# A two-layer hybrid diffusion block: norms as one unbroken VectorE sequence, seams reordered

## The chip, the cores and the metric

The kernel runs on one core of a Trainium2 chip. The metric is device time in microseconds (us) of one execution, as the median of several runs. TensorE multiplies matrices, VectorE and ScalarE work element by element, GpSimd and SyncE issue transfers (GpSimd does a little arithmetic as well). In the profile they are called PE, DVE, ACT, POOL and SP.

## The reference

512 latent tokens and 256 context tokens of width 1024 pass through two layers. In each layer the input is normed and modulated, projected once, and the projection is cut into a bidirectional linear recurrence (A), a spatial gating MLP (B), a windowed attention with a sink (C) and three gates. The last layer updates latent tokens alone.

```python
zx = modulate(rms_norm(x, g_norm1[l]), sh1x, sc1x) @ w_in[l]
ya_x = rglru_bidir(zx[..., OFF_A:OFF_B], ...)
yb_x = spatial_gating(gelu(zx[..., OFF_B:OFF_Q]), ...)
yc_x = windowed_attention(q, k, v, kc, vc, sink[l])
x = x + ga1x * merge_branches(zx[..., OFF_G:], ya_x, yb_x, yc_x, w_branch[l], w_out[l])
x = x + ga2x * sq_relu_mlp(modulate(rms_norm(x, g_norm2[l]), sh2x, sc2x), w_ff1[l], w_ff2[l])
```

`rms_norm` divides by the root of the mean square over the 1024 channels of a token. `modulate` is `h * (1 + scale) + shift`, and scale, shift and the gates `ga1`, `ga2` come from a product of the conditioning vector with `w_mod`. Everything is 32-bit floating point.

## The kernel before

**Products.** Channels lie on the 128 partitions, tokens along the free dimension: `self.x` is 8 tiles of 128 channels by 768 tokens (512 in the last layer). A 32-bit product is made of three passes: both operands are split into a high part (a copy rounded to fp32r) and a low part (the rest), and high by high, high by low and low by high are summed in PSUM. A weight block is 128 x 1024 elements. `parted` (L193 and below in `Net`) loads it on SP (`wr<-w`), copies the high part on ACT (`wh<-wr`) and subtracts on DVE (`wl<-wr,wh`). There are three buffers each for `wr`, `wh` and `wl`. One block against one range of tokens is 24 passes of TensorE. 44 blocks of layer 1 (`EARLY`, the four key/value blocks first) are split ahead of time during the MLP of layer 0, stored by GpSimd as `hd` and `ld`, and later loaded back by SP straight into `wh` and `wl`.

**Order.** Nothing is issued as the code is read. Each call is recorded, and `schedule` then plans all five engines: at each moment an engine takes the recorded operation with the best priority that is ready by the planner's costs, fits the buffers, and lies within `far` (275) operations of the oldest unfinished one. A transfer is taken to land 1900 ns after its bytes have passed at 360 bytes/ns. `emit` issues the planned order, so every instruction of the trace has one source line, L508. Calls within `bundle()` are planned as one piece, with nothing of the same engine between them. In `rsqrt` (nine to twelve tiny DVE operations, Newton's method) only the tags in `CHAINS` are bundled.

**Norms.** `rms` sums squares: ACT squares, DVE adds over the 8 tiles, PE adds over partitions (matmuls of one column). On DVE follow the mean, the root, and for every 128 tokens one diagonal matrix (`s<-ident,t`). PE spreads the diagonals over the partitions with a matmul by ones (`p<-s,ones`). `norm` then multiplies by that and by the gain (DVE, `s<-s,G,p`), and ACT and DVE make the high and low parts that the next product reads. Between the diagonals and the first product of the next stage lies that whole chain.

**Seams.** To give TensorE work in the meantime, the two products next to a norm run on one range of tokens after the other ("streams", `streams(W)`: 512 and 256 tokens in layer 0, 256 and 256 in layer 1). `out_proj` does 2 of its 8 blocks on all tokens at once and 6 per stream, and norms a stream when it is done. `ff` does the first group of four blocks of its first matrix per stream, everything in the middle on all tokens, and in layer 0 the last group `ff2(7)` per stream, each followed by the norm of layer 1; then come the keys and values of layer 1 (`kv_proj`). Between the streams of a seam the same weight block is loaded and split anew.

**Other work in the gaps.** `merge` adds the three gated branch projections. DVE also computes the modulation of later stages as 128 dot products of a row of `w_mod` with the conditioning vector (`junk<-wr,condb`, the row loaded by SP as `wr<-wmod`). `layer_consts` loads and prepares the recurrence's constants of a layer, and `kv_post` calls it at the layer's start.

Of the kernel before, what the change touches and what calls it, by code (L numbers as in the profile page):

```python
# [19 lines left out]
F32R = mybir.dt.float32r  # L20
# [3 lines left out]
OP = mybir.AluOpType  # L24
# [33 lines left out]
LAZY = 200  # L58
DRAINS = 50
FULL, URGENT = 6, 150  # L60
WINDOW = 275
TABLES = {"Sigmoid": (2,), "Sqrt": (3,), "Gelu_apprx_tanh": (11,), "Exp": (0,), "Tanh": (0, 2, 11)}

# [119 lines left out]
class Rec:  # L183
# [153 lines left out]
    def schedule(self):  # L337
# [90 lines left out]
        while events:  # L428
            now = events[0][0]
            while events and events[0][0] <= now + 1e-6:  # L430
                _, _, kind, x = heapq.heappop(events)
                if kind == "rel":
                    used[x.tag] -= 1
                    places[x.tag].append(x)
                    live[x.tag][x.first:x.last + 1] -= 1
                    if x.early:
                        early[x.tag][x.early[0]:x.early[1]] -= 1
            for e in range(5):
                while free[e] <= now + 1e-6:
                    best = pick(e)  # L440
                    if best is None:
                        break
                    _, j, i = best
                    cand[e].pop(j)
                    op = ops[i]
                    for b in op.new:
                        if b.space == "dram":
                            continue
                        used[b.tag] += 1
                        b.early = None  # L450
                        b.prev = places[b.tag].pop(0)
                        if b.prev is None:
                            b.place = fresh[b.tag]
                            fresh[b.tag] += 1
                        else:
                            b.place = b.prev.place
                        if b.first > front:
                            b.early = (front, b.first)
                            early[b.tag][front:b.first] += 1
                    dur = op.dur  # L460
                    if op.both and free[POOL] > now and busy:
                        dur += free[POOL] - now
                    if e == POOL:
                        busy = not op.nbytes
                    if e == ACT and op.table and table not in op.table:
                        dur += 1283
                        table = op.table[0]
                    free[e] = now + dur
                    end = now + dur
                    if op.nbytes:  # L470
                        dma = max(dma, end) + op.nbytes / 360.0
                        end = dma + 1900
                    op.end = end
                    for b in op.psum:
                        b.acc[e] = end
# [46 lines left out]
AHEAD_C = ('', '0', '1', '2', 'k', '')  # L522
AHEAD_X = ('', '0', '1', 'k')
NEAR = 60
JOINT = (2,)
EARLY = [*range(B_K, B_F2), *range(B_G, B_P), *range(B_AX, B_V)]


# [1 line left out]
class Net:  # L530
# [43 lines left out]
    def weights(self, l, blk):  # L574
        rec = self.rec
        rec.boost, was = self.wboost, rec.boost
        if (l, blk) in self.stored:
            hi = self.wtile("wh", [128, 1024], F32R)
            lo = self.wtile("wl", [128, 1024], F32R)
            for t, d in zip((hi, lo), self.stored[l, blk]):  # L580
                rec.sync.dma_start(t.bitcast(F32), d.bitcast(F32))
        else:
            hi, lo = self.parted(l, blk)
        rec.boost = was
        return hi, lo
# [67 lines left out]
    def begin(self, hs):  # L653
# [8 lines left out]
        G = self.hold([128, 2, KT], F32, name="G00", tag="G0")  # L662
        ps = [self.p1() for _ in range(6)]
        self.wboost = 0
        for k in range(KT):
            if k % 2 == 0:
                p = self.mod_rows(k // 2)
                w = self.weights(0, B_K + k // 2)
            nc.vector.tensor_scalar(G[:, :, k], p[:, 2 * (k % 2):2 * (k % 2) + 2], bm[:, k:k + 1],
                                    vec[:, V_G1 + k:V_G1 + k + 1], op0=OP.add, op1=OP.mult)  # L670
# [142 lines left out]

    def rms(self, parts, adder=None):
        nc = self.nc
        sums = []
        for i, (a, b) in enumerate(parts):
            S = self.slot([128, b - a])
# [14 lines left out]
                                     start=True, stop=True)  # L833
                    n += 1
        v = self.tiny(nt, "nv")
        nc.vector.tensor_scalar(v, ps[:, :nt], 1.0 / D, EPS, op0=OP.mult, op1=OP.add)
        rs = self.rsqrt(v, nt, "n")
        out = []
        n = 0
        for a, b in parts:  # L840
            dg = self.slot([128, b - a])
            for i in range((b - a) // 128):
                nc.vector.tensor_scalar(dg[:, i * 128:(i + 1) * 128], self.ident, rs[:, n:n + 1], None, op0=OP.mult)
                n += 1
# [106 lines left out]
    def kv_post(self, l, ps, pairs):  # L951
        nc = self.nc
        if pairs[0] == 0:
            self.layer_consts(l)
            self.kr, self.VS = [], []
        n = 8 * len(pairs)
        ss = self.tiny(n, "kss")
# [443 lines left out]
    def ff(self, l, hs, W):  # L1401
        nc = self.nc

        def ff1(c, parts):
            out = [(self.slot([128, W], F32R), self.slot([128, W], F32R)) for _ in range(4)]
            for z in parts:
                for j in range(4):
                    w = self.weights(l, B_F1 + 4 * c + j)
                    if len(parts) == 1:
                        self.ahead()  # L1410
                    ps = self.fm(w, hs, z)
                    for p, a, b in ps:
                        r = self.slot([128, b - a])
                        nc.scalar.activation(r, p, AF.Relu)
                        nc.vector.tensor_mul(r, r, r)
                        self.split(r, out[j][0][:, a:b], out[j][1][:, a:b])
            return out

        def ff2(c, z, parts):
            for j in range(4):  # L1420
                w = self.weights(l, B_F2 + 4 * c + j)
                if c < 7:
                    self.ahead()
                for i in range(2):
                    ps = self.fm(w, z, parts, kk=4, off=i * 128, stride=256)
                    self.residual(l, 40, ps, 2 * j + i)

        z = ff1(0, [[q] for q in self.streams(W)])
        self.aside = False
        for c in range(7):  # L1430
            for _ in range(3):
                self.bg()
            z2 = ff1(c + 1, [self.parts(W)])
            ff2(c, z, self.parts(W))
            z = z2
        if l == DEPTH - 1:
            ff2(7, z, self.parts(W))
            return
# [7 lines left out]
        for toks in (range(4), range(4, 6)):  # L1446
            self.kv_proj(l + 1, hs, ps, toks)
            self.kv_post(l + 1, ps, (0, 1) if toks[0] == 0 else (2,))
        return hs, ps

    def run(self):
        nc, t = self.nc, self.t
        self.setup()
        hs = self.pairs(TOK)
        ps = self.begin(hs)
        self.consts()
        self.xsrc = t["x"]
        for l in range(DEPTH):
            last = l == DEPTH - 1
# [141 lines left out]
```

## Time and profile before

| | |
|---|---|
| median of 3 runs | 2654.45 us (2653.88 to 2655.54) |
| profiled execution | 2655.47 us, span 2653.7 us |
| TensorE busy | 2604.5 us, 98% of the span |
| VectorE, ScalarE, GpSimd busy | 1840.1, 1200.1, 122.7 us |
| mean granted TensorE clock | 0.995 of full speed |
| 336 loads `wr<-w` of 512 KB | 3.8 us from issue to landing (median) |
| transfers | 403.54 MB, 152 GB/s over the span |

Times are from the start of the span. A row of the timeline gives start, duration, engine, source line, operation, output and inputs, shape and count; in brackets stands how long the engine had been idle before it and what ended that. Buffer numbers are left out there, so that all weight blocks read `wl<-wr,wh`. "Granted clock" is TensorE's clock in parts of full speed; its two levels are 1.2 and 2.4 GHz, that is 0.5 and 1.0. `SPq` is the transfer itself, `SP` its issue.

### The profile page before, as it was taken

What the parts mean: (1) busy time and instruction counts of PE and PEld (TensorE: products, weight loads), DVE (VectorE), ACT (ScalarE), POOL (GpSimd) and SP (SyncE); (2) the same over time, 40 slices, a digit from 0 to 9 for tenths busy, and PEclk for the clock granted to TensorE, in tenths of its full rate; (3) what the DMA queues carried; (4) which work ended last, traced back from release to release, by engine and by line L of the source; (5) the groups of instructions that cost most, each with busy time, mean ns of one, the idle gap of its engine ahead of it and who ended that gap; (6) DMA issues with size and microseconds to landing.
All of it is one profiled execution on the core that took longest, in us unless ns stands there. A gap on an engine that the chain in (4) does not pass through costs nothing.

```text
span 2653.7 us, 38578 instructions
## 1 busy us (share of the span) xinstructions
PE 2604.5 (98%) x14916; PEld 2246.2 (85%) x14916; DVE 1840.1 (69%) x3504; ACT 1200.1 (45%) x1987; POOL 122.7 (5%) x217
## 2 busy tenths in 40 slices
PE   7999999999999999999999989999999999999999
PEld 4989988888898888888888878888887888888887
DVE  8888776997637748465666678886986567844444
ACT  4566557993122225332333334667993233532322
POOL 1000000011000000100111000000011000000000
PEclk9999999999999999999999999999999999999999
DMA  6122213466425424766778634334577565533332
GB/s 248 45 69 74 61 56 104 122 198 226 154 80 165 162 79 134 230 214 199 246 261 263 207 134 169 105 121 154 159 245 248 165 189 178 158 95 96 95 93 83
DMA packets 129528, 403.54 MB, mean 152 GB/s; under 512 B 15232, under 2 KB 25632, under 8 KB 129344
## 3 DMA queue, kind: packets, MB, share of 16 engines
q1 hardware_dynamic: 99360, 302.11, 36.3%
q0 software_dynamic: 23072, 83.24, 9.4%
q10 hardware_dynamic: 6912, 15.73, 1.6%
q8 instruction: 117, 1.92, 0.3%
q14 instruction: 67, 0.55, 0.1%
HBM read 319.23 MB, written 81.79 MB: 151 GB/s over the span
## 4 chain that ended last, share of the span: by engine, by line
PE 69%; DVE 6%; ACT 3%; issue 1%; DMA 1%; ACTq 0%; DVEq 0%; POOLq 0%
PE p L508 69%; DVE s L508 4%; ACT s L508 3%; DVE wl L508 1%; DMA wr<-wmod 1%; DVE t L508 1%; ACT L508 0%; ACT wh L508 0%; DMA ya<-s 0%; DVE junk L508 0%; ACTq L508 0%; DVEq L508 0%; POOLq L508 0%
## 5 line engine op out<-in xcount | busy, mean ns | idle before, releaser
L508 PE MATMUL p<-s,wh 128*128 128x512 f32 (+1 forms) x6816 | 1670.7, 353 | 8.8 <-DVE s L508 6.1
L508 PEld LDWEIGHTS p<-s,wh 128*128 128x128 f32 x6816 | 1192.0, 189 | 239.7 <-DVE s L508 7.8
L508 PE MATMUL p<-s,wl 128*128 128x512 f32 (+1 forms) x3408 | 1028.5, 351 | 8.8 <-DVE wl L508 8.8
L508 ACT ACTIVATE wh<-wr 128x1024 fp32r<-128x1024 f32 x336 | 354.8, 1059 | 871.7 <-PE p L508 475.0
L508 PEld LDWEIGHTS p<-s,wl 128*128 128x128 f32 x3408 | 570.3, 189 | 58.2 <-DVE wl L508 11.1
L508 DVE TENSOR_TENSOR wl<-wr,wh 128x1024 fp32r<-128x1024 f32 x336 | 409.7, 1222 | 291.8 <-ACT wh L508 249.6
L508 ACT ACTIVATE s<-p 128x512 f32<-128x512 f32 (+6 forms) x598 | 282.0, 511 | 271.1 <-PE p L508 255.2
L508 PE MATMUL p<-wh,s 128*128 128x256 f32 (+1 forms) x1472 | 301.9, 298 | 1.7 <-DVE s L508 1.0
L508 DVE TENSOR_TENSOR s<-s,s 128x512 fp32r<-128x512 f32 (+5 forms) x361 | 258.1, 728 | 53.4 <-ACT s L508 49.0
L508 PE MATMUL p<-s,s 128*128 128x256 f32 (+3 forms) x1568 | 279.9, 319 | 5.9 <-ACT s L508 3.9
L508 ACT ACTIVATE s<-s 128x512 fp32r<-128x512 f32 (+6 forms) x301 | 182.5, 633 | 195.7 <-DVE s L508 179.3
L508 PEld LDWEIGHTS p<-s,s 128*128 128x128 f32 (+1 forms) x1568 | 219.5, 183 | 41.0 <-DVE s L508 7.3
L508 PEld LDWEIGHTS p<-wh,s 128*128 128x128 f32 x1472 | 236.3, 188 | 13.7 <-DVE s L508 2.3
L508 DVE SCALAR_TENSOR_TENSOR s<-p,mod,s 128x512 f32<-128x512 f32 (+1 forms) x222 | 138.7, 646 | 156.2 <-PE p L508 155.5
L508 PE MATMUL p<-wl,s 128*128 128x256 f32 (+1 forms) x736 | 217.9, 296 | 1.0 <-DVE wl L508 1.0
L508 DVE SCALAR_TENSOR_TENSOR junk<-wr,condb 128x1024 bf16<-128x1024 f32 x128 | 156.4, 1222 | 86.7 <-DMA wr<-wmod 85.7
L508 DVE TENSOR_TENSOR s<-p,s 128x512 fp32r<-128x512 f32 (+4 forms) x324 | 182.8, 595 | 37.3 <-ACT s L508 31.5
L508 PEld LDWEIGHTS p<-wl,s 128*128 128x128 f32 x736 | 138.5, 188 | 6.6 <-DVE wl L508 1.6
L508 ACT ACTIVATE s<-s,t,t 128x512 f32<-128x512 f32 (+1 forms) x128 | 109.9, 863 | 50.2 <-DVE t L508 49.8
L508 DVE SCALAR_TENSOR_TENSOR s<-s,s 128x768 f32<-128x768 f32 x128 | 116.7, 949 | 16.2 <-ACT s L508 16.2
L508 PE MATMUL p<-ident,s 128*128 128x128 f32 (+1 forms) x776 | 102.9, 274 | 5.2 <-DVE s L508 3.1
L508 PEld LDWEIGHTS p<-ident,s 128*128 128x128 f32 (+1 forms) x776 | 88.4, 142 | 14.1 <-ACT s L508 3.5
(90 smaller groups left out, 1236.2 us busy)
## 6 DMA issues: line engine op xcount, KB each, us to landing
wr<-w SPq DMA_DIRECT2D x336, 512.0 KB, 3.8
wr<-wmod SPq DMA_DIRECT2D x80, 512.0 KB, 4.2
wl<-ld SPq DMA_DIRECT2D x48, 512.0 KB, 4.8
wh<-hd SPq DMA_DIRECT2D x48, 512.0 KB, 3.7
hd<-wh POOLq DMA_DIRECT2D x44, 512.0 KB, 3.7
ld<-wl POOLq DMA_DIRECT2D x44, 512.0 KB, 5.6
gd<-s ACTq DMA_DIRECT2D x24, 384.0 KB, 2.6
s<-gd POOLq DMA_DIRECT2D x24, 384.0 KB, 5.7
```

Source lines behind the costliest of these rows:

```text
L508: ins = getattr(getattr(self.nc, name), method)(*[r(x) for x in a], **{q: r(x) for q, x in k.items()})
```

## The change

1. `rms`: mean, root and all diagonals of a norm are one bundle (`WHOLE`), and the diagonals' buffers are taken first.
2. `schedule`: a transfer is taken to land 2600 ns (SP, ACT) or 4800 ns (POOL) after its bytes, rather than 1900 ns (`LANDS`).
3. `weights`: loads of split key/value blocks are planned only within 160 operations of the oldest unfinished one (`CLOSE`).
4. `ff`: in layer 0 the last seam does blocks 2 and 3 of `ff2(6)` per stream as well (`SPLIT`, `THIRDS`); in layer 1 the first seam also does blocks 0 and 1 of the second column group per stream (`OVER`).
5. `out_proj`: 1 block jointly and 7 per stream, rather than 2 and 6 (`JOINT`).
6. `layer_consts` of layer 1 is called in the middle of layer 0's MLP (`CONSTS`); that of layer 0 and `consts` get a range of 200 rather than 275 (`LATE`).
7. `begin`: the first gain columns are computed ahead of the loop (`LEAD`).

```diff
@@ globals
+LANDS = {SP: 2600, ACT: 2600, POOL: 4800}
-JOINT = (2,)
+CLOSE = 160
+CONSTS = 4
+LEAD = 1
+LATE = 200
+WHOLE = True
+SPLIT = 2
+OVER = (0, 1)
+THIRDS = ((0, 512), (512, 768))
+JOINT = (1,)
@@ schedule
-                        end = dma + 1900
+                        end = dma + LANDS[e]
@@ weights
+            rec.far = CLOSE if B_K <= blk < B_Q else None
             for t, d in zip((hi, lo), self.stored[l, blk]):
                 rec.sync.dma_start(t.bitcast(F32), d.bitcast(F32))
+            rec.far = None
@@ begin
+        for pair in range(LEAD):
+            scales(pair)
         for k in range(KT):
             if k % 2 == 0:
-                p = self.mod_rows(k // 2)
+                if k // 2 >= LEAD:
+                    scales(k // 2)
                 w = self.weights(0, B_K + k // 2)
@@ rms
-        nc.vector.tensor_scalar(v, ps[:, :nt], 1.0 / D, EPS, op0=OP.mult, op1=OP.add)
-        rs = self.rsqrt(v, nt, "n")
+        dgs = [self.slot([128, b - a]) for a, b in parts]
...
+        with self.rec.bundle() if whole else nullcontext():
+            if whole:
+                nc.vector.tensor_scalar(v, ps[:, :nt], 1.0 / D, EPS, op0=OP.mult, op1=OP.add)
+                rs = self.rsqrt(v, nt, "nn")
+            n = 0
+            for dg, (a, b) in zip(dgs, parts):
+                for i in range((b - a) // 128):
+                    nc.vector.tensor_scalar(dg[:, i * 128:(i + 1) * 128], self.ident, rs[:, n:n + 1], None, op0=OP.mult)
+                    n += 1
@@ kv_post
-            self.layer_consts(l)
+            if l == 0:
+                self.rec.far = LATE
+                self.layer_consts(l)
+                self.rec.far = None
@@ ff
-        z = ff1(0, [[q] for q in self.streams(W)])
+        z, z1 = room(), room() if l == DEPTH - 1 else None
+        for q in self.streams(W):
+            ff1(0, [q], z)
+            if z1:
+                ff1(1, [q], z1, OVER)
...
+            if c == CONSTS and l < DEPTH - 1:
+                rec = self.rec
+                rec.boost, was = -LAZY, rec.boost
+                self.layer_consts(l + 1)
+                rec.boost = was
+            if c == 0 and z1:
+                z2 = ff1(1, self.parts(W), z1, [j for j in range(4) if j not in OVER])
+            else:
+                z2 = ff1(c + 1, self.parts(W), room())
+            ff2(c, z, self.parts(W), range(4) if c < 6 or l == DEPTH - 1 else range(SPLIT))
+            z, z6 = z2, z
...
-        for q in self.streams(W):
+        for q in THIRDS:
+            ff2(6, z6, [q], range(SPLIT, 4))
             ff2(7, z, [q])
             self.norm(l + 1, 0, hs, G, *q)
```

What this does to the order of the instructions is seen best at three places. The first is SP's queue at the seam between the layers. `wr` are blocks of the last MLP group, `ld_112`, `hd_112` and the next numbers the parts of the stored key/value blocks. Before:

```order
L508 DMA wr_14727<-w 128x1024
L508 DMA wr_14765<-w 128x1024
L508 DMA wl_14789<-ld_112_10941 128x1024
L508 DMA wh_14793<-hd_112_10919 128x1024
L508 DMA wr_14821<-w 128x1024
L508 DMA wl_14877<-ld_113_11019 128x1024
L508 DMA wr_14949<-w 128x1024
L508 DMA wr_14988<-w 128x1024
L508 DMA wr_15028<-w 128x1024
L508 DMA wr_15068<-w 128x1024
L508 DMA wr_15110<-w 128x1024
L508 DMA wh_15225<-hd_113_11000 128x1024
```

Now:

```order
L509 DMA wr_14919<-w 128x1024
L509 DMA wr_14958<-w 128x1024
L509 DMA wr_14998<-w 128x1024
L509 DMA wr_15040<-w 128x1024
L509 DMA wl_15066<-ld_112_10960 128x1024
L509 DMA wr_15139<-w 128x1024
L509 DMA wl_15166<-ld_113_11038 128x1024
L509 DMA wh_15207<-hd_112_10944 128x1024
L509 DMA wh_15259<-hd_113_11028 128x1024
L509 DMA wh_15381<-hd_114_11110 128x1024
```

The loads of blocks 112 and 113 stood ahead of the last five or six weight loads and now stand among the last two; two more weight blocks are loaded, because two blocks of `ff2(6)` come once per stream.

The second place is DVE at the first norm of layer 1's MLP (the stream of tokens 0 to 255). `t` are mean and root, `s<-ident,t` the diagonals, `wl` splits of weight blocks, `s<-s,G,p` the norm's products. Before, from the root's end on:

```order
L508 SCALAR_TENSOR_TENSOR t_22453<-t_22451,t_22453 128x2
L508 TENSOR_TENSOR wl_22478<-wr_22359,wh_22435 128x1024
L508 TENSOR_SCALAR s_22492<-ident,t_22453 128x128
L508 SCALAR_TENSOR_TENSOR s_21502<-p_22431,mod_10721,s_21502 128x256
L508 TENSOR_SCALAR s_22492<-ident,t_22453 128x128
L508 TENSOR_TENSOR wl_22506<-wr_22394,wh_22487 128x1024
L508 SCALAR_TENSOR_TENSOR s_22516<-s_21496,G_22031,p_22511 128x256
L508 SCALAR_TENSOR_TENSOR s_22523<-s_21498,G_22031,p_22511 128x256
L508 SCALAR_TENSOR_TENSOR s_22530<-s_21500,G_22031,p_22511 128x256
```

Now:

```order
L509 SCALAR_TENSOR_TENSOR t_22463<-t_22461,t_22463 128x2
L509 TENSOR_SCALAR s_22476<-ident,t_22463 128x128 x2
L509 TENSOR_TENSOR wl_22499<-wr_22374,wh_22450 128x1024
L509 SCALAR_TENSOR_TENSOR s_22512<-s_21501,G_22099,p_22507 128x256
L509 TENSOR_TENSOR wl_22519<-wr_22409,wh_22505 128x1024
L509 SCALAR_TENSOR_TENSOR s_22532<-s_21503,G_22099,p_22507 128x256
L509 SCALAR_TENSOR_TENSOR s_22542<-s_21508,G_22099,p_22507 128x256
L509 SCALAR_TENSOR_TENSOR s_22550<-s_21512,G_22099,p_22507 128x256
```

A weight split and a residual stood among root and diagonals; now nothing does, and the splits follow.

The third place is DVE in layer 1's merge of branch A. `junk` is a modulation dot product that waits for a row of `w_mod`, `s<-s,s` are the low parts of the branch's 8 tiles, which the first product of the merge reads. Before:

```order
L508 TENSOR_TENSOR s_20482<-s_19995,s_20255 128x512
L508 TENSOR_TENSOR s_20489<-s_20026,s_20480 128x512
L508 TENSOR_TENSOR s_20498<-s_20063,s_20487 128x512
L508 SCALAR_TENSOR_TENSOR junk,mod_10721<-wr_20467,condb 128x1024
L508 TENSOR_TENSOR wl_20521<-wr_20462,wh_20493 128x1024
L508 TENSOR_TENSOR s_20537<-s_20086,s_20507 128x512
L508 SCALAR_TENSOR_TENSOR s_20363<-s_20363,p_20472 128x512
L508 TENSOR_TENSOR s_20551<-s_20096,s_20515 128x512
L508 TENSOR_TENSOR s_20556<-s_20113,s_20519 128x512
L508 TENSOR_TENSOR s_20561<-s_20167,s_20530 128x512
```

Now:

```order
L509 TENSOR_TENSOR s_20521<-s_20045,s_20495 128x512
L509 TENSOR_TENSOR s_20530<-s_20075,s_20505 128x512
L509 TENSOR_TENSOR wl_20539<-wr_20479,wh_20516 128x1024
L509 TENSOR_TENSOR s_20548<-s_20102,s_20512 128x512
L509 SCALAR_TENSOR_TENSOR s_20385<-s_20385,p_20487 128x512
L509 TENSOR_TENSOR s_20560<-s_20109,s_20532 128x512
L509 TENSOR_TENSOR s_20567<-s_20131,s_20541 128x512
L509 TENSOR_TENSOR s_20572<-s_20207,s_20543 128x512
L509 TENSOR_TENSOR s_20577<-s_20497,s_20565 128x512
L509 SCALAR_TENSOR_TENSOR junk,mod_10735<-wr_20500,condb 128x1024
L509 SCALAR_TENSOR_TENSOR s_20507<-s_20507,p_20552 128x512
```

The dot product stood ahead of a weight split and four low parts, and now stands behind all of them.

## Rows read from the trace of the kernel before

**Rows 1.** The page: span, and busy time of each engine.
```profile
span 2653.7 us, 38578 instructions
...
PE 2604.5 (98%) x14916; PEld 2246.2 (85%) x14916; DVE 1840.1 (69%) x3504; ACT 1200.1 (45%) x1987; POOL 122.7 (5%) x217
```

**Rows 2.** TensorE's waits, 1510 to 1570 us: total, times, longest.
```profile
PE p L508 <- DVE wl L508: 8.8, 7, 2.5
PE p L508 <- DVE s L508: 1.0, 1, 1.0
```

**Rows 3.** Timeline of SP, 1499 to 1512 us.
```profile
1500.87 0.33 SPq L508 DMA_DIRECT2D wl<-ld  x1
...
1509.27 0.32 SPq L508 DMA_DIRECT2D wl<-ld  x1
```

**Rows 4.** Timeline of the seam between the layers, 1524 to 1560 us.
```profile
1524.48 1.06 ACT L508 ACTIVATE wh<-wr 128x1024 fp32r<-128x1024 f32 x1 [1.42 <-PE p L508]
...
1525.77 0.50 PE L508 MATMUL p<-s,wl 128*128 128x512 f32 x1 [0.92 <-DVE wl L508]
...
1556.37 2.07 DVE L508 SCALAR_TENSOR_TENSOR s<-s,G,p 128x512 f32<-128x512 f32 x3 [0.77 <-PE p L508]
...
1559.62 0.38 PE L508 MATMUL p<-s,wl 128*128 128x256 f32 x1 [1.65 <-DVE wl L508]
```

**Rows 5.** Windows: busy of PE, PEld, DVE, ACT, POOL; granted clock; DMA.
```profile
383.00:390.00 7.00, 6.41 (x33) 5.72 (x34) 5.57 (x12) 5.52 (x13) 0.00 (x0) 0.76 0.00 0
1512.00:1552.00 40.00, 33.42 (x163) 26.56 (x161) 23.61 (x52) 11.82 (x15) 4.33 (x8) 1.00 0.36 120
1552.00:1556.00 4.00, 3.43 (x13) 2.84 (x13) 2.51 (x8) 0.79 (x2) 0.00 (x0) 0.57 0.00 0
2044.00:2052.00 8.00, 6.52 (x18) 5.10 (x19) 6.27 (x10) 1.06 (x1) 1.08 (x2) 0.58 0.90 318
2300.00:2308.00 8.00, 6.37 (x34) 6.37 (x35) 5.02 (x14) 2.48 (x6) 0.00 (x0) 0.58 0.14 55
2308.00:2312.00 4.00, 4.00 (x36) 4.00 (x35) 3.01 (x4) 2.58 (x6) 0.00 (x0) 1.00 0.25 74
```

**Rows 6.** TensorE's waits, 2290 to 2305 us.
```profile
PE p L508 <- DVE s L508: 3.4, 2, 2.2
PE p L508 <- ACT s L508: 1.7, 1, 1.7
```

**Rows 7.** Timeline of DVE at layer 1's second norm.
```profile
2291.86 0.15 DVE L508 TENSOR_SCALAR t<-p 128x2 f32<-128x2 f32 x1
...
2294.64 1.22 DVE L508 TENSOR_TENSOR wl<-wr,wh 128x1024 fp32r<-128x1024 f32 x1
...
2297.97 3.21 DVE L508 SCALAR_TENSOR_TENSOR s<-s,G,p 128x256 f32<-128x256 f32 x8
```

**Rows 8.** Timeline in layer 1's merge of branch A.
```profile
2037.26 6.78 SPq L508 DMA_DIRECT2D wr<-wmod  x2
...
2042.45 1.22 DVE L508 SCALAR_TENSOR_TENSOR junk<-wr,condb 128x1024 bf16<-128x1024 f32 x1 [2.82 <-DMA wr<-wmod]
...
2045.48 0.80 PE L508 MATMUL p<-s,wh 128*128 128x512 f32 x1 [3.32 <-DVE s L508]
```

**Rows 9.** Timeline at the end of layer 0's attention.
```profile
377.24 1.23 DVE L508 TENSOR_TENSOR wl<-wr,wh 128x1024 fp32r<-128x1024 f32 x1 [2.96 <-ACT wh L508]
...
378.58 0.92 ACT L508 ACTIVATE s<-s,t,t 128x640 f32<-128x640 f32 x1 [1.37 <-DVE t L508]
...
383.46 1.79 PE L508 MATMUL p<-ident,s 128*128 128x128 f32 x10 [2.36 <-DVE s L508]
```

**Rows 10.** TensorE's waits at layer 0's second norm, 1000 to 1030 us.
```profile
PE p L508 <- DVE s L508: 1.3, 3, 0.6
```

**Rows 11.** Timeline of the first norm, 18 to 21 us.
```profile
18.12 1.50 PE L508 MATMUL p<-ones,s 128*128 128x1 f32 x12 [1.60 <-DVE s L508]
...
20.57 0.16 DVE L508 TENSOR_SCALAR t<-p 128x6 f32<-128x6 f32 x1
```

More of the change, by code (lines that the diff above doesn't have):

```diff
@@ L664, in begin, with scales @@
         self.wboost = 0
+        def scales(pair):
+            p = self.mod_rows(pair)
+            for k in (2 * pair, 2 * pair + 1):
+                nc.vector.tensor_scalar(G[:, :, k], p[:, 2 * (k % 2):2 * (k % 2) + 2], bm[:, k:k + 1],
+                                        vec[:, V_G1 + k:V_G1 + k + 1], op0=OP.add, op1=OP.mult)
+        for pair in range(LEAD):
+            scales(pair)
         for k in range(KT):
             if k % 2 == 0:
-                p = self.mod_rows(k // 2)
+                if k // 2 >= LEAD:
+                    scales(k // 2)
                 w = self.weights(0, B_K + k // 2)
-            nc.vector.tensor_scalar(G[:, :, k], p[:, 2 * (k % 2):2 * (k % 2) + 2], bm[:, k:k + 1],
-                                    vec[:, V_G1 + k:V_G1 + k + 1], op0=OP.add, op1=OP.mult)
             self.mod_cols(k)
@@ L815, in rms @@
         nc = self.nc
+        whole = adder is not None or WHOLE
         sums = []
@@ L835, in rms @@
         v = self.tiny(nt, "nv")
-        nc.vector.tensor_scalar(v, ps[:, :nt], 1.0 / D, EPS, op0=OP.mult, op1=OP.add)
-        rs = self.rsqrt(v, nt, "n")
-        out = []
[L839 to L844, printed above, removed]
+        dgs = [self.slot([128, b - a]) for a, b in parts]
+        if not whole:
+            nc.vector.tensor_scalar(v, ps[:, :nt], 1.0 / D, EPS, op0=OP.mult, op1=OP.add)
+            rs = self.rsqrt(v, nt, "n")
+        with self.rec.bundle() if whole else nullcontext():
+            if whole:
+                nc.vector.tensor_scalar(v, ps[:, :nt], 1.0 / D, EPS, op0=OP.mult, op1=OP.add)
+                rs = self.rsqrt(v, nt, "nn")
[4 more added lines that the diff above has]
+                    n += 1
+        out = []
+        for dg, (a, b) in zip(dgs, parts):
             p = self.p1()
@@ L1402, in ff, with room, ff1, ff2 @@
         nc = self.nc
[L1404 to L1416, printed above, removed]
-            return out
-        def ff2(c, z, parts):
-            for j in range(4):
+        def room():
+            return [(self.slot([128, W], F32R), self.slot([128, W], F32R)) for _ in range(4)]
+        def ff1(c, parts, out, js=range(4)):
+            for j in js:
+                w = self.weights(l, B_F1 + 4 * c + j)
+                if len(parts) == len(self.parts(W)):
+                    self.ahead()
+                ps = self.fm(w, hs, parts)
+                for p, a, b in ps:
+                    r = self.slot([128, b - a])
+                    nc.scalar.activation(r, p, AF.Relu)
+                    nc.vector.tensor_mul(r, r, r)
+                    self.split(r, out[j][0][:, a:b], out[j][1][:, a:b])
+            return out
+        def ff2(c, z, parts, js=range(4)):
+            for j in js:
                 w = self.weights(l, B_F2 + 4 * c + j)
@@ L1432, in ff @@
                 self.bg()
-            z2 = ff1(c + 1, [self.parts(W)])
-            ff2(c, z, self.parts(W))
-            z = z2
+            if c == CONSTS and l < DEPTH - 1:
[9 more added lines that the diff above has]
+            z, z6 = z2, z
         if l == DEPTH - 1:
@@ L1442, in ff @@
         ps = [self.p1() for _ in range(6)]
-        for q in self.streams(W):
+        for q in THIRDS:
+            ff2(6, z6, [q], range(SPLIT, 4))
             ff2(7, z, [q])
             self.norm(l + 1, 0, hs, G, *q)
-        for toks in (range(4), range(4, 6)):
-            self.kv_proj(l + 1, hs, ps, toks)
-            self.kv_post(l + 1, ps, (0, 1) if toks[0] == 0 else (2,))
+        for a, b in THIRDS:
+            self.kv_proj(l + 1, hs, ps, range(a // 128, b // 128))
+            self.kv_post(l + 1, ps, tuple(range(a // 256, b // 256)))
         return hs, ps
@@ L1455, in run @@
         ps = self.begin(hs)
+        self.rec.far = LATE
         self.consts()
+        self.rec.far = None
         self.xsrc = t["x"]
```

## The prediction

> **What bounds the kernel now.** I read the page first. TensorE is busy for 2604.5 of 2653.7 us [rows 1]: the program is one long queue of matmuls, and no other engine is above 69%. So the time is TensorE's work, plus what it stands still (49.2 us), plus what its work is stretched where the granted clock falls. The change adds no columns to any product; it can gain only from the last two. Next I went through TensorE's waits by stretch and looked for each at the engine that ended it. Five places hold most of what can be moved:
>
> - the seam between the layers: 8.8 + 1.0 us, nearly all for weight splits [rows 2];
> - the MLP norm of layer 1: 3.4 + 1.7 us [rows 6];
> - the merge of branch A in layer 1: one wait of 3.32 us [rows 8];
> - the end of layer 0's attention: one wait of 2.36 us [rows 9];
> - the MLP norm of layer 0: 1.3 us [rows 10].
>
> That is 21.9 us. Of the remaining 27.3 us much is the start, the end after the last matmul, and small waits that have no common cause.
>
> Last I read the granted clock around them. While TensorE waited seven times for about 0.9 us, from 1512 to 1552, the clock stayed at 1.00 [rows 4, 5]. Behind each of the four longer waits it fell to 0.5 for a few microseconds, so that the windows show 0.76, 0.57, 0.58 and 0.58 [rows 5]. I take busy time times (1 - clock) as the loss: 6.41 x 0.24 = 1.5, 3.43 x 0.43 = 1.5, 6.52 x 0.42 = 2.7, 6.37 x 0.42 = 2.7. Together 8.4 us that no table of waits shows.
>
> The Trainium skill (TensorE: Matmul & The Clock Gate, HAM oscillation) says that long pauses of TensorE send its clock from 2.4 back to 1.2 GHz, and that a kernel pays this at each such pause; the trace agrees with 8.4 us at four places. The same page (What's actually happening) says that what the gate goes by runs freely, not from the program's start, so that the same pause need not cost the same twice; by that a pause of 1.65 us left at a seam may still cost the 1.5 us that I count as returned, and the sum below would be 1.5 to 3 us smaller.
>
> **The change part by part**, in time of the profiled run.
>
> *Seam between the layers.* SP fetches the stored parts of the first two key/value blocks at 1500.87 and 1509.27 [rows 3], but they are read only behind the last wait here, after 1559.62 [rows 4]. They sit in two of the three low-part buffers. So each block of the last MLP group must wait until TensorE lets go of the one buffer left: ACT makes the high part at 1524.48 on TensorE's release, DVE follows, and TensorE stands still 0.92 us for the low part at 1525.77 [rows 4]; so at each block. `CLOSE` moves these loads behind all but the last weight loads, which removes the cause for about the first ten of its twelve blocks. The root and its four diagonals, into which DVE had put a split, now come in one piece, and `SPLIT` puts six blocks of the narrow stream (6 x 24 passes) in front of them rather than four. What is late next: once the two loads are issued, the last two or three splits are again held to one buffer, and one of them stands behind four products of 512 columns of the norm. Three such took 2.07 us before a split, and TensorE waited 1.65 us for it [rows 4]. I leave 1.65 for this one, 0.85 for the other splits and the first low part: 2.5 us (between 1.0, if only the last wait of rows 2 stays, and 6). Clock: 1.5 back. Gain 9.8 + 1.5 - 2.5 = 8.8.
>
> *MLP norm of layer 1.* From the mean at 2291.86 the chain of small operations runs to 2294.64, where a weight split of 1.22 us comes between root and diagonals; after the diagonals another stands ahead of the norm's eight products (3.21 us) [rows 7]. All that time TensorE has only four blocks of the other stream. 36 narrow matmuls take 4.00 us from 2308 on [rows 5], 0.111 each, so four blocks of 24 are 10.7 us. `OVER` makes them six: 16.0 us, 5.3 more than now, against 5.1 us of waits. The bundle brings the diagonals forward by the split and a residual, 1.6 us. Against this, DVE is already full there: it is busy for the 3.21 us and what follows, and each of the two new blocks brings it a split of 1.22 us and more. I followed the new order of DVE with these durations and come out level with TensorE, within a microsecond. I leave 0.6 us (0 to 4). Gain 5.1 + 2.7 - 0.6 = 7.2.
>
> *Merge of branch A.* A dot product stands ahead of a weight split and of four low parts that the merge's first product reads. Its row of `w_mod` was issued at 2037.26; DVE idled 2.82 us for it, and TensorE 3.32 us behind that [rows 8]. In the new order the dot product follows all eight low parts. The row is no earlier, but beside it now lies work: five low parts and splits, and then TensorE's first block. What is late next is the low parts themselves, which follow one another on DVE. I leave 1.5 us (0.5 to 4). Gain 3.3 + 2.7 - 1.5 = 4.5.
>
> *End of attention.* A split that idles 2.96 us for its high part stands in the middle of the softmax on DVE, and the exponentials start at 378.58 [rows 9]. Now the split stands behind the row maxima. ACT's copy for the same weights still precedes the exponentials, so only the split and the idle time behind that copy go: 377.24 against 378.58, 1.3 us. I expect about 1 us of the wait left and the clock to be kept in part: gain 2.0 (0 to 3.9).
>
> *MLP norm of layer 0.* Of 1.3 us [rows 10], which come from a split among the diagonals, 0.4 stays: 0.9. `JOINT` puts one block more into each stream there and in layer 1; it lengthens the cover by a block and costs a load and a split, hidden (below).
>
> *Start.* TensorE has summed the squares at 18.12 + 1.50 = 19.62, but DVE takes the mean at 20.57, behind constants of the recurrence [rows 11]. `LATE` and the bundle remove that 0.95 us, and the loads of constants that GpSimd issued meanwhile compete less with `x`. What is late next are rows of `w_mod`. I take 1.0 (-1 to 2.5).
>
> *What is added.* Six more weight blocks are loaded and split: 6 x 1.06 us on ACT, 6 x 1.22 us on DVE [rows 4, 7]. Neither is the bound, and the transfers of a whole run keep the queues half empty (DMA share 0.36 in the 40 us at the seam [rows 5]): cost zero, and up to 7.3 us if DVE is full at each of them. `layer_consts` of layer 1 moves into the middle of layer 0's MLP, among blocks that run on all tokens at once and give DVE the most time per split: zero. The passes that go from 512 to two of 256 columns have the same columns: zero.
>
> *What is disturbed.* The longer assumed landing reorders every engine over the whole program. At the places above I trust each hand count to about 1 us, and errors there add waits more often than they take them away; elsewhere small waits move about. I take 4 us against the change (from -4, all small ones gone, to +12).
>
> Sum: 8.8 + 7.2 + 4.5 + 2.0 + 0.9 + 1.0 - 4 = 20.4 us. The profiled run was 2655.5 us (its span 2653.7 and 1.8 around it), so 2635.1; the median shown lies 1.0 below the profiled run, which I leave within the rounding: **2635 us**.
>
> **Rivals.**
>
> *Only the two big seams pay.* The merge, the attention's end and the start keep their waits in other clothes, since the transfers behind them (the 2037.26 issue took 5 us) are no shorter. Then 8.8 + 7.2 + 0.9 - 4 = 12.9 us: 2642. For it speaks that a late transfer is only passed to the next reader; against it that both waits came from the place of one instruction in DVE's queue.
>
> *The gains are spent.* The buffers at the layer seam are held as before: the planner still lets one key/value load out before the last splits, and if one of the first of them gets its buffer only then, the 0.9 us waits come back at each of twelve blocks (about 6 to 8 us remain of 11.3). With 3 us from the other norm and 4 from the rest, less 4 for disturbance: about 2648 to 2655, no change to be measured. This is also the case that the change does not do what it says. Against it: all but one of the last weight loads now precede them.
>
> *Slower: DVE becomes the bound at the narrow streams.* A narrow block is 24 x 0.111 = 2.7 us of TensorE, and asks of DVE one split of 1.22 us, two residual updates of about 0.40 us and, where a norm gathers its squares, two additions; beside it lie sixteen products and low parts of the other stream. At the layer seam (0.65 to 0.69 us each at 512 columns, from 2.07 for three [rows 4]) these alone are 11 us in a stretch of 16. With six splits (7.3), twelve updates (4.8) and eight additions (3.2 at most) that is 26 us of DVE. From the point where DVE needs over 2.7 us a block, each further block waits: 26 against 16 us, plus 1.5 to 2.7 of clock, would be some 13 us at the layer seam instead of 11.3, 10 instead of 7.8 at the norm of layer 1, 4 instead of 1.3 at that of layer 0, and with 4 of disturbance and no gain elsewhere: 2655.5 + 1.7 + 2.2 + 2.7 + 4 = 2666. For it speaks that DVE is the releaser of most of these waits; against it that the next product, the keys and values, needs no split and lets DVE catch up while it runs (96 wide passes, each twice 0.111 us, 21 us).
>
> **How the numbers follow.** My forecast case (2627 to 2639) 0.62; only the seams (2639 to 2646) 0.20; spent 0.11; slower 0.07. A measurement here tells 0.2%, that is 5.3 us, from no change: faster means under 2649.1. Parts of the spent case lie just under this line. Faster 0.84, same 0.10, slower 0.06. The range runs from 2626 (all small waits gone as well, about 29 us) to 2649, which leaves out the slower case and most of the spent one.
>
> **What would show it.** Right: TensorE's waits at the layer seam fall from 9.8 to about 2.5 us, and no wait for a weight split of about 0.9 us repeats there; at the MLP norm of layer 1 less than 1 us is left and the clock stays at 1.00; in the merge the dot product's idle time is no longer followed by a wait of TensorE over 1.5 us. Busy time of TensorE falls by about 8 us, as the clock is kept. Wrong: if DVE's share in the narrow streams is full and TensorE waits there for low parts at each block; if the half clock stays where waits shrank; or if new waits over 1 us appear in attention, recurrence or merges and add up to more than 6 us.

## The result and the profile after

The changed kernel takes 2624.65 us (median of 4 runs, 2623.34 to 2625.87), the kernel before 2654.16 us (4 runs beside it): a ratio of 0.9891 (95% interval 0.9874 to 0.9908). That is 29.5 us faster by the medians, 28.9 by the ratio. The forecast was 2635 us with a range down to 2626: the sign and the places were right, the size was a third too small, and the time lies 1.35 us below the range.

The profiled execution took 2625.87 us. Its page, to be held against [rows 1]:

```profile
span 2624.0 us, 38741 instructions
...
PE 2599.0 (99%) x14988; PEld 2246.4 (86%) x14988; DVE 1850.9 (71%) x3515; ACT 1205.6 (46%) x1998; POOL 122.6 (5%) x217
```

The span is shorter by 29.7 us: TensorE stands still 24.2 us less (25.0 against 49.2, each the span less TensorE's busy time), and its busy time falls by 5.5 us although it has 72 more instructions. The second part is clock: 8.4 us came back and 1.6 were lost anew (both below); the added instructions may account for the rest of the difference. What TensorE still waits for, in the whole run (releaser, total, times, longest):

```profile
PE p L509 <- DVE s L509: 8.8, 10, 4.5
PE p L509 <- ACT s L509: 4.9, 5, 1.9
PE p L509 <- DMA s<-wmod_k: 3.4, 2, 2.8
PE p L509 <- DVE wl L509: 1.9, 2, 1.6
PE p L509 <- ACT wh L509: 1.1, 1, 1.1
```

The same view in stretches: at the end of attention (370 to 390), at layer 0's MLP norm (990 to 1030) and in the merge (2010 to 2050) it has no row left. At the layer seam (1510 to 1570), at layer 1's MLP norm (2255 to 2290) and at the start (0 to 60, three rows) it has, in this order:

```profile
PE p L509 <- DVE wl L509: 1.6, 1, 1.6
...
PE p L509 <- DVE s L509: 0.2, 1, 0.2
...
PE p L509 <- DVE s L509: 6.5, 3, 4.5
PE p L509 <- DMA s<-wmod_k: 3.4, 2, 2.8
PE p L509 <- ACT s L509: 1.0, 2, 0.5
```

The windows that answer to [rows 5], around the same work (columns as there; the granted clock is the third figure from the right), with one that is new:

```profile
378.00:385.00 7.00, 6.86 (x45) 5.61 (x44) 5.57 (x12) 6.55 (x15) 0.00 (x0) 1.00 0.00 0
446.00:450.00 4.00, 3.97 (x14) 3.41 (x15) 3.97 (x6) 4.00 (x9) 0.00 (x0) 0.60 0.01 2
1500.00:1540.00 40.00, 40.00 (x202) 33.31 (x201) 26.87 (x49) 14.04 (x17) 4.33 (x8) 1.00 0.55 188
1544.00:1552.00 8.00, 8.00 (x56) 7.29 (x57) 8.00 (x13) 4.17 (x7) 0.00 (x0) 1.00 0.27 102
2026.00:2034.00 8.00, 8.00 (x36) 6.48 (x35) 6.59 (x11) 1.69 (x2) 2.14 (x4) 1.00 0.95 339
2274.00:2282.00 8.00, 8.00 (x69) 8.00 (x68) 8.00 (x16) 6.72 (x14) 0.00 (x0) 1.00 0.62 182
```

All four places run at full speed now. One half-clock stretch is new, behind a wait of 1.88 us in the recurrence of layer 0 (446 us): 3.97 x 0.40 = 1.6 us.

The timeline of the layer seam shows why. SP first, then DVE, then TensorE's one wait:

```profile
1531.59 0.33 SPq L509 DMA_DIRECT2D wl<-ld  x1
...
1538.22 0.33 SPq L509 DMA_DIRECT2D wl<-ld  x1
...
1540.02 2.73 DVE L509 SCALAR_TENSOR_TENSOR s<-s,G,p 128x512 f32<-128x512 f32 x4
1542.66 1.22 DVE L509 TENSOR_TENSOR wl<-wr,wh 128x1024 fp32r<-128x1024 f32 x1
...
1543.94 0.39 PE L509 MATMUL p<-s,wl 128*128 128x256 f32 x1 [1.57 <-DVE wl L509]
```

The stored low parts are fetched some 30 us later than in [rows 3], although the seam itself now comes sooner, and the wait that the prediction left, a split behind norm products, is there: 1.57 us. In the merge the dot product that stood among the low parts now follows the eighth of them and has its row without waiting:

```profile
2022.70 2.15 DVE L509 TENSOR_TENSOR s<-s,s 128x512 fp32r<-128x512 f32 x3 [1.19 <-PE p L509]
...
2027.11 2.49 DVE L509 TENSOR_TENSOR s<-s,s 128x512 fp32r<-128x512 f32 x4
2029.52 1.22 DVE L509 SCALAR_TENSOR_TENSOR junk<-wr,condb 128x1024 bf16<-128x1024 f32 x1
```

In the kernel before, three low parts stood ahead of this dot product and five (not four) behind it. Dot products ahead of all the low parts still idle for their rows (2.13 us before the one at 2014.84), as they did before the change (2.68 us before the one at 2025.31); in neither profile does TensorE wait behind those.

### The profile page after: what moved, and what is told of

It is laid out like the page before. It is cut to its first block, busy times and chain, and to the rows that moved or that the text cites. A ratio compares the mean times of both kernels' runs of the same rounds, so it can differ in the third digit from the quotient of the medians.

```text
span 2624.0 us, 38741 instructions
## 1 busy us (share of the span) xinstructions
PE 2599.0 (99%) x14988; PEld 2246.4 (86%) x14988; DVE 1850.9 (71%) x3515; ACT 1205.6 (46%) x1998; POOL 122.6 (5%) x217
## 5 line engine op out<-in xcount | busy, mean ns | idle before, releaser
L509 ACT ACTIVATE wh<-wr 128x1024 fp32r<-128x1024 f32 x342 | 361.4, 1059 | 853.9 <-PE p L509 655.3
L509 DVE TENSOR_TENSOR wl<-wr,wh 128x1024 fp32r<-128x1024 f32 x342 | 417.6, 1222 | 241.6 <-ACT wh L509 236.8
```

Source lines behind the costliest of these rows:

```text
L509: ins = getattr(getattr(self.nc, name), method)(*[r(x) for x in a], **{q: r(x) for q, x in k.items()})
```

## The experiments

Each kernel was timed in rounds with the kernel before on the same chip; ratios are to that. The kernel before took 2650.9 to 2652.2 us in these rounds, so the changed kernel's 0.9891 is what the first five are held against. A distance from the changed kernel is given by the medians, with the distance by the ratios behind it where the two differ by over 1 us.

**Assumed landings back.** `LANDS = {SP: 1900, ACT: 1900, POOL: 1900}` in the changed kernel.

> The changed kernel, with the assumed landing back at 1900 ns for all queues; everything else as changed. Theory A (the assumed landing moved the dot product of the merge and the split of the softmax, and their waits go with that alone): the wait of 3.3 us in layer 1's merge of branch A and the one of about 2.4 us at the end of layer 0's attention come back, each with a stretch of half clock (2.7 and 1.5 us): 7 to 10 us slower than the changed kernel, about 2633 us. Both big seams keep what they gained: under 3 us of waits at the layer seam, under 1 us at layer 1's MLP norm. Rival B (these two places were freed by the other edits, or by chance of the new plan): within 3 us of the changed kernel.

Measured: 2634.74 us, ratio 0.9936 (0.9921 to 0.9950), 10 us slower than the changed kernel (12 by the ratios). The merge has its wait back, with the dot product ahead of the low parts:

```profile
2028.67 1.23 DVE L509 SCALAR_TENSOR_TENSOR junk<-wr,condb 128x1024 bf16<-128x1024 f32 x1 [2.69 <-DMA wr<-wmod]
...
2031.70 0.52 PE L509 MATMUL p<-s,wh 128*128 128x512 f32 x1 [2.49 <-DVE s L509]
...
2031.00:2036.00 5.00, 4.30 (x11) 3.12 (x12) 4.63 (x8) 0.00 (x0) 1.07 (x2) 0.66 0.88 335
```

The window's clock of 0.66 adds 1.5 us. At the end of attention 1.17 us came back rather than 2.4, with no half clock, and the start took 2.6 us more waits (13.5 against 10.9). Theory A holds in full for the merge and by half for the attention; about half of the price lies where it had not been expected, at the start and in small waits.

**Stored loads free again.** `CLOSE = 275` in the changed kernel.

> The changed kernel, with the stored key/value loads planned within 275 operations as before. Theory A (these loads hold two of three low-part buffers, and that made the 0.9 us waits): they return at the last five to eight blocks of the layer seam, 5 to 9 us of waits for weight splits there instead of 1.6, so 4 to 8 us slower, about 2631 us. Rival B (the longer narrow stream and the unbroken norm freed the seam): at most 2 us slower, no repeated wait of 0.9 us.

Measured: 2635.09 us, ratio 0.9936 (0.9921 to 0.9950), 10 us slower (12 by the ratios). TensorE's waits, 1500 to 1560 us, and the clock of the last part:

```profile
PE p L509 <- DVE wl L509: 5.7, 6, 1.1
PE p L509 <- DVE s L509: 2.5, 1, 2.5
...
1543.00:1551.00 8.00, 6.04 (x24) 5.00 (x25) 6.61 (x17) 3.72 (x6) 0.00 (x0) 0.57 0.22 66
```

The repeated waits of 0.85 to 1.1 us are back (8.2 us against 1.6) with 6.04 x 0.43 = 2.6 us of half clock. That is 6.6 + 2.6 = 9.2 us more, over Theory A's 4 to 8: the last waits are longer than the block-by-block ones, and the clock comes on top. About 2 us more of this profile lie at the start and are not the edit's (last section). Rival B falls: the longer narrow stream alone does not free the seam.

**Mean, root and diagonals apart again.** `WHOLE = False` in the changed kernel.

> The changed kernel, with mean, root and diagonals planned apart, as before (the root alone stays one piece). Theory A (the unbroken sequence only takes out one or two splits per norm, and the longer narrow streams cover the rest): 1 to 3 us slower, waits of 0.5 to 1 us at the MLP norm of layer 0 and up to 1 us at that of layer 1, about 2627 us. Rival B (the unbroken sequence is the main source of the gain at the norms): 6 us or more slower, with waits of TensorE at three or more norms and half clock behind them.

Measured: 2623.34 us, ratio 0.9893 (0.9878 to 0.9908): no difference from the changed kernel. At layer 1's MLP norm 0.6 us of waits in place of 0.2 (first row), at layer 0's 0.4 in place of none (second):

```profile
PE p L509 <- DVE s L509: 0.6, 2, 0.4
...
PE p L509 <- DVE s L509: 0.4, 2, 0.2
```

Beside the longer streams the unbroken sequence is worth less than can be told here. Rival B falls; Theory A's 1 to 3 us do not show either, though noise could hide them. The unbroken sequence was not tried on the kernel before alone, so what it is worth with short streams is open.

**Lengths of the narrow streams back.** `SPLIT = 4`, `OVER = ()`, `JOINT = (2,)` in the changed kernel; and, in a later round, `OVER = ()` alone.

> The changed kernel, with the lengths of the narrow streams as before (no second group of blocks at layer 1's first MLP seam, none of the group before the last at the layer seam, two joint blocks of the output projection). Theory A (layer 1's MLP norm waited for want of work for TensorE): 3 to 5 us of waits return there with 2.7 us of half clock, and 1 to 2 us at the layer seam: 6 to 9 us slower, about 2632 us. Rival B (the unbroken sequence and the moved loads suffice, the extra blocks only load DVE): within 2 us of the changed kernel, or faster.

> The changed kernel, with only the second group of blocks at layer 1's first MLP seam taken out of the narrow streams; the two other lengths stay as changed. Theory A (these two blocks are what covers layer 1's MLP norm): waits of 2.5 to 4.5 us return there, with 1.5 to 2.7 us of half clock, 4 to 6 us slower than the changed kernel. Rival B (the one block more of the output projection covers it): under 1.5 us of waits there, at most 2 us slower.

Measured: 2630.67 us, ratio 0.9924 (0.9908 to 0.9941) for all three, 6 us slower (9 by the ratios); 2629.26 us, ratio 0.9916 (0.9902 to 0.9929) for `OVER` alone, where the changed kernel ran in the same round with 0.9898 (2623.84 us), so 5.4 us slower. TensorE's waits at layer 1's MLP norm (2255 to 2290) of the second, and the clock behind them:

```profile
PE p L509 <- DVE s L509: 3.5, 2, 3.3
PE p L509 <- ACT s L509: 0.6, 1, 0.6
...
2274.00:2280.00 6.00, 5.23 (x31) 5.23 (x32) 4.83 (x13) 1.67 (x5) 0.00 (x0) 0.72 0.29 87
```

With all three undone it is 4.0 us there, and 3.0 instead of 1.6 at the layer seam. So `OVER` alone carries layer 1's norm (4.1 us of waits and 5.23 x 0.28 = 1.5 us of clock), as Theory A said. What `SPLIT` and `JOINT` are worth together is not shown: the two medians differ by 1.4 us, in different rounds and within the noise.

**The start's order back.** `LATE = 275`, `LEAD = 0` in the changed kernel.

> The changed kernel, with the first layer's constants and the first gain columns planned as before (range 275, nothing ahead of the loop). Theory A (what the start gained comes from the constants' transfers standing behind the additions on GpSimd): the first key/value product begins 1 to 3 us later and the kernel is 1 to 4 us slower, about 2627 us; nothing after 60 us moves by more than 1 us. Rival B (the start gained by the assumed landing or by chance of the clock): within 1 us.

Measured: 2626.29 us, ratio 0.9906 (0.9891 to 0.9921), 1.6 us slower (4 by the ratios), which is within the noise. TensorE's waits up to 60 us add up to 14.1 us, as before the change, against 10.9:

```profile
PE p L509 <- DVE s L509: 12.6, 3, 7.1
PE p L509 <- ACT s L509: 1.5, 1, 1.5
```

Theory A's 3 us are there in the waits, and the start loses still more, because the half clock holds longer there: 13 to 24 us and 34 to 38 us show 0.53 and 0.59, where the changed kernel had half clock from 13 to 17 us alone. As a mark behind the start I take the 600th matmul of a trace (up to it all these kernels have the same matmuls but for two): it begins at 126.92 us here, in the changed kernel at 121.52 and in the kernel before at 123.62. The total hides this by luck: this profile lacks the half clock behind the wait at 446 us and the changed kernel's wait of 1.7 us at 1960, so something after 60 us did move. Without `LANDS` (first experiment) the 600th matmul begins at 124.96 us, and with `LANDS` alone (next experiment) at 124.43. By these single profiles the start needs both, the later constants and the longer landing; the same order alone spreads over 2.3 us (last section).

**The two main edits on the kernel before, apart and together.** `LANDS` in `schedule`; `CLOSE = 160` in `weights`; both.

> The kernel before, with the assumed landings of 2600 and 4800 ns alone. Theory A (this edit alone frees the merge and the end of the attention): the waits of 3.3 and 2.4 us and their half clock go, TensorE's waits at the layer seam (9.8 us) and at layer 1's MLP norm (5.1 us) stay: 7 to 11 us faster than before, ratio about 0.9965. Rival B (it only reorders, and gains one wait for another): within 3 us of before, ratio 0.999 to 1.001.

> The kernel before, with the stored key/value loads held to a range of 160 alone. Theory A (this edit alone ends the repeated waits of the layer seam): no wait of about 0.9 us repeats there, 2 to 4 us of waits stay for the norm, and the rest of the program keeps its waits: 6 to 9 us faster than before, ratio about 0.997. Rival B (without the two blocks more in the narrow stream the norm is uncovered and takes what is gained): within 3 us of before.

> The kernel before, with both of these edits and none of the rest. Theory A (the two are independent): their gains add up, 14 to 20 us faster than before, ratio 0.9925 to 0.9945; what the changed kernel has beyond that are the longer streams (about 6 us) and the start. Rival B (they overlap, both freeing low-part buffers): less than 12 us faster.

Measured: `LANDS` alone 0.9960 (0.9945 to 0.9975), `CLOSE` alone 0.9974 (0.9964 to 0.9985), both 0.9932 (0.9917 to 0.9947). The product of the two is 0.9934: they add up, 10.6 and 6.9 us against 18.0. TensorE's waits at the layer seam (1500 to 1565), of the first two in this order:

```profile
PE p L509 <- DVE wl L509: 7.8, 6, 2.5
PE p L509 <- DVE s L509: 1.0, 1, 1.0
...
PE p L508 <- DVE wl L508: 3.4, 2, 1.7
PE p L508 <- DVE s L508: 0.6, 1, 0.6
```

`LANDS` leaves the seam nearly as it was (8.8 us against 9.8) and empties the merge and the end of attention (no row in either); `CLOSE` leaves these two (3.0 and 2.3 us) and more than halves the seam. Between both (0.9932) and the changed kernel (0.9891, later 0.9898) 9 to 11 us remain. Some 5 of them are `OVER` (fourth experiment), and about 4 show at the start of the two profiles: with both edits the 600th matmul begins at 125.49 us, behind half clock from 13 to 30 us, in the changed kernel at 121.52. How much of these 4 us is order and how much the clock's chance is not separated. What the other edits add is within the noise.

**Can the seam's last wait go?** Range 110 for the stored key/value blocks and the query blocks, so that none is fetched before the last weight block of the MLP; then the same with `WHOLE = False`; beside them the changed kernel again.

```diff
-CLOSE = 160
+CLOSE = 110
-            rec.far = CLOSE if B_K <= blk < B_Q else None
+            rec.far = CLOSE if B_K <= blk < B_F2 else None
```

> The changed kernel itself once more, beside the next three on the same chip: both theories, ratio to the kernel before within its first interval, 0.987 to 0.991.

> The changed kernel, with the range of stored loads at 110 instead of 160, for the query blocks of layer 1 as well as for its key/value blocks, so that no stored block is fetched before the last weight load of the MLP. Theory A (the last wait of the layer seam, 1.57 us, comes from the two stored low parts that still precede the last splits): it falls under 0.6 us, and the kernel is 1 to 2 us faster than the changed one, 2623 us. Rival B (the split waits behind the norm's products on DVE whatever the buffers): the wait stays over 1.2 us. Rival C (the stored blocks come too late now): a wait for a load of 1 us or more at the first key/value product, slower by 1 to 3 us.

> The same, and with mean, root and diagonals planned apart again. Theory A (the unbroken sequence is worth nothing once the streams are longer): within 2 us of the run before it. Rival B (with the seam's last wait gone the norm's chain is what is late, and splits among it show): 2 us or more slower, with waits at the diagonals of 0.5 us or more.

Measured: changed kernel 2623.84 us, ratio 0.9898 (0.9882 to 0.9913), as before; range 110 2639.51 us, 0.9956 (0.9943 to 0.9968); with the sequence broken 2640.49 us, 0.9959 (0.9947 to 0.9972). The sequence is again worth nothing, as its Theory A said. For the range, Theory A was right on the wait of 1.57 us, which is gone, and wrong on the time: a larger wait stands 15 us on, and it is not the wait for a load that Rival C named. DVE, then TensorE, then the window:

```profile
1548.30 4.72 DVE L509 SCALAR_TENSOR_TENSOR s<-s,mod,s 128x512 fp32r<-128x512 f32 x7
...
1553.98 2.05 DVE L509 SCALAR_TENSOR_TENSOR s<-p,mod,s 128x256 f32<-128x256 f32 x5
1555.95 3.59 DVE L509 TENSOR_TENSOR s<-s,s 128x256 f32<-128x256 f32 x7
...
1559.60 1.02 PE L509 MATMUL p<-ones,s 128*128 128x1 f32 x4 [8.47 <-DVE s L509]
...
1551.00:1565.00 14.00, 5.53 (x16) 4.44 (x16) 10.38 (x33) 2.40 (x6) 0.00 (x0) 0.63 0.21 78
```

TensorE has been given only three passes of the key/value product (24 in the changed kernel) before the column sums of the second stream, and those wait for all of DVE's backlog: the norm's low parts of the first stream, five residual updates, seven additions. The stored blocks are not what it waits for. With them fetched later, the plan put the products that should cover this backlog behind the sums. A backlog on DVE at the layer seam is what the slower rival named, though here it comes as one wait and not one at each block: 8.5 us and 5.53 x 0.37 = 2.0 us of clock, and 4.6 us of small waits from 1600 to 1850 (one of 1.18 us at 1629 among them); the rival had put 13 us at the seam. Whether the smaller range or the query blocks did this was not tried apart. No version beat the changed kernel clear of noise.

## Why the prediction was right in kind and too small

Each term of the sum against the two profiles (waits plus half clock before, less what is left):

| place | forecast | measured |
|---|---|---|
| seam between the layers | 8.8 | 11.3 - 1.6 = 9.7 |
| MLP norm of layer 1 | 7.2 | 7.8 - 0.2 = 7.6 |
| merge of branch A | 4.5 | 6.0 |
| end of attention | 2.0 | 3.9 - 0.1 = 3.8 |
| MLP norm of layer 0 | 0.9 | 1.3 |
| start | 1.0 | 14.1 - 10.9 = 3.2 |
| disturbed elsewhere | -4 | 29.7 - 31.6 = -1.9 |
| sum | 20.4 | 29.7 (span) |

- **The step that failed is what I left at each place.** Every term was reckoned from waits that were really there, and the mechanisms of the seam, the merge and layer 1's norm were each confirmed by an experiment. But I put a remainder behind each place, and only the seam's was real. These remainders make 5.0 of the 9.3 us that the sum is short, the start 2.2 and the charge for disturbance 2.1. In the merge I left 1.5 us for the low parts following one another: none is left, since the dot product now stands behind all of them. At the attention's end I let ACT's copy still hold the exponentials and counted 1.3 us: the exponentials start at 373.74 and TensorE arrives at 378.68; before it was 378.58 against 381.10. That is 2.4 us more lead, and the wait of 2.36 is gone with its clock.
- **The range.** Its low end took all small waits as gone, about 29 us, and counted them from the profiled run, as the forecast did; the 1 us by which the median lies below the profiled run was left out. Here the profiled run took 2625.87 us and the median is 1.2 us lower: nearly all of the 1.35 us by which the range was missed.
- **The seam.** I counted seven waits of about 0.9 us. The trace of the kernel before has five (0.85 to 1.09 us, 4.6 us together); the other two for weight splits are 2.52 us, ahead of 1552.57, and the 1.65 us that I named. `CLOSE` alone took the five away and left 4.0 of 9.8 us, so the cause was right but carried about half of the price that I put on it; the changed kernel's other edits took off the rest, down to 1.57 us.
- **The start** was sized by one interval, 0.95 us behind the constants. That interval closed (sums at 17.11 + 1.50, mean at 18.71), but the first product of diagonals by ones also begins 3.1 us sooner (22.17 against 25.29) and the squares' sum 1.0 us sooner (17.11 against 18.12). The fifth and the first experiment show two edits behind this; my term knew one. In time the start gained 2.1 us (the 600th matmul), less than the 3.2 in its waits.
- **The charge for disturbance** was taken from hand counts that I trusted to a microsecond each, and all of them on the dear side. What `LANDS` did disturb is the recurrence of layer 0: the wait at 446 us (1.43 to 2.01 us) stands in all eleven profiles with the longer landing and in none of the three with 1900 ns, which instead have two waits of 0.92 to 1.27 us between 534 and 562 us. Of the 1.9 us measured, 1.6 are the half clock behind this wait. The wait of 1.7 us at 1960 in this profile is not in the changed kernel's second one, so it does not belong to the order.
- **Attribution.** For the two MLP norms I counted the unbroken sequence among the causes. Beside the longer streams it is not one: without it the time is the same. `OVER` covers layer 1's norm. At layer 0's the waits of 1.3 us are there with `LANDS` alone and with `LANDS` and `CLOSE`, 0.4 is left without the unbroken sequence and nothing without the longer streams: either of the two takes most of it. With the old lengths the sequence may be worth something. From the kernel before with both main edits to the changed kernel with the old lengths, which has the sequence, the waits at layer 1's norm go from 4.9 to 4.0 us; but the two also differ in the start and the constants.
- **Rivals.** That only the big seams pay fell with the empty rows in the merge and at the attention's end; that the buffers stay held fell with the seam's one remaining wait. The slower rival did not occur in the change, but a backlog on DVE at the seam can: the run with range 110 met one.
- **The clock.** I counted 8.4 us and got them; a new stretch of 1.6 took some back. For the thought that the same pause need not cost the same twice I had named the Trainium skill (TensorE: Matmul & The Clock Gate, What's actually happening), by which what the gate goes by runs freely. The traces agree: at 446 us a wait of 1.88 us was followed by half clock in one profile and one of 1.91 us in another was not. The seam's remaining 1.57 us cost none.
- `CONSTS` was not tried alone.

## What to carry to other kernels

Where one engine is busy for 98%, list its idle times and the half-clock stretches behind them, and ask for each whose place in which queue caused it. The five places found so hold 28.4 of the 31.6 us in the table, and a single planning constant moved two of them. At four of these five the wait, caused by a place in a queue, went away nearly whole once the place changed: leave a remainder only where a named instruction still stands in front. And moving a load later frees its buffer only as long as the work that needs it does not move behind something slower: a range of 160 operations gained 7 us on the kernel before, one of 110 (with the query blocks) lost 16 against it in the changed kernel.

## What the runs showed of the hardware

The same instructions in the same order had different starts. The kernel with the stored loads free has, on every engine, the changed kernel's order until shortly before the layer seam (1499 us), yet its half clock at the start held for about 14 us, not 4. The window of it, and that of the changed kernel:

```profile
13.00:29.00 16.00, 14.89 (x43) 6.57 (x44) 11.92 (x36) 5.25 (x11) 5.23 (x7) 0.57 1.05 389
```

```profile
13.00:17.00 4.00, 3.30 (x8) 0.86 (x8) 3.69 (x4) 2.54 (x8) 3.67 (x5) 0.57 1.04 394
```

The last start-up product that waits begins at 34.48 us in the one and at 32.21 in the other, and the 600th matmul at 123.79 and 121.52. In all, eight profiles share their order on every engine up to 945 us; in the other seven the first half-clock stretch lasts 3.4 us (three) or 6.8 us (four), and the 600th matmul begins at 121.52 to 121.85. Part of the spread between runs (2646 to 2655 us of the kernel before) may come from here; that was not tested. And the same wait, that in layer 0's recurrence at 446 us, was followed by half clock where it lasted 1.83, 1.88 and 2.01 us, but not where it lasted 1.91, nor in seven profiles where it lasted 1.43 to 1.74.
